# S5 chunk states and outputs: inputs and states as the stationary operand, tables as the moving one

## The chip, the cores and the metric

The kernel runs on one NeuronCore of a Trainium2 chip. The metric is the device time of one launch in microseconds (us). Three runs of the kernel before took 1204.42 to 1205.73 us, median 1205.5.

The engines are named as the profile names them: PE is TensorE (matrix products), PEld its weight loads, DVE is VectorE, ACT is ScalarE, POOL is GpSimd, SP is the engine that issues the loads from memory. In a matrix product one operand is stationary (it is loaded into the array as weights, [contracted rows, output rows]) and the other is moving (it streams past, one column after another).

## The reference

Four layers on x of 256 tokens by 1024 channels, each a token mixer followed by a squared-ReLU MLP of width 4096, both with a pre-norm and a residual addition. Layers 0 and 3 mix with S5, layer 1 with differential attention, layer 2 with pooling. S5, cut to what matters here (64 groups of 16 channels, 64 complex states each; the scan runs over tokens):

```python
u = h @ w_in                                   # 256 x 1024, read as 64 groups of 16 channels
# for each group g and token t, x complex with 64 entries:
#   x[t] = abar * x[t-1] + bbar @ u[t]
y = jnp.einsum('btgp,ghp->btgh', xr, c_re) - jnp.einsum('btgp,ghp->btgh', xi, c_im)
y = y + d_skip * u
z = jax.nn.gelu(y)
z = z * jax.nn.sigmoid(z @ w_gate)
return z @ w_out
```

## The kernel before, in words

**Chunks of four tokens.** The kernel doesn't scan over 256 tokens. It cuts them into 64 chunks of 4. For a pair of groups (2 x 16 channels) an input column holds the 4 x 32 = 128 inputs of one chunk, so a pair has a matrix V of 128 rows by 64 chunks. With tables that are built from the parameters: S (`st`) leads from the inputs of a chunk to the state that the chunk adds (128 = two groups x 64 states, once for the real and once for the imaginary part); T leads from the inputs to the outputs of the same chunk; O leads from the state before the chunk to the outputs. The states are carried from chunk to chunk by VectorE: a rotation by phases (`ph`) makes the recurrence real, two TENSOR_TENSOR_SCAN instructions run it, and a rotation back gives h, the state before each chunk.

**Quarters.** The 32 pairs of groups are taken in four quarters of eight pairs. The steps for a quarter q, each one letter: g the product with W_in (two halves of the contracted dimension), V the scaling and the transposes into V, m (`s5_state`) the chunk states, c (`s5_chain`) the carries, y (`s5_out`) the outputs and the Gelu, z (`s5_z`) the transposes of z into rows of channels. For a half n of the columns e is the product with W_gate (four units) and w that with W_out. The tables: p parameters, i input table, o output table, s phases and decays, S the transposes that make `st` (`states`, copies in L598), T the products that make T (`outputs`, L613 to L626), and f transposes of x.

Layer 0 makes all its tables beside its own work. Those of layer 3 are made during the MLPs ahead, in pieces, and are kept in memory; K, H and L (`s5_get`) bring back the tables of m, of c and of y by loads that SP issues. There are two buffers each of `st`, O and T (q even, q odd), so a table of quarter q can be written when the stage of quarter q - 2 that reads it is over.

**The order** of the steps is written out by hand in the strings `SEQ[0]` and `SEQ[1]` (L87 to L89; layers 0 and 3); every engine gets its instructions in that order. A step's instructions stand in the engines' lists at the place of the step, so an instruction that waits holds up what stands behind it on its engine. Weights come in half blocks of 256 x 512 (or whole 128 x 1024 pieces) that SP loads ahead in the order of use, and that ScalarE and VectorE split into a rounded part and the rest (`fetch`); three products of these parts make one product in float32's precision. The products of m, y, S and T are plain float32 products instead: in the trace each is two PE instructions. All matrix products are recorded under L142, transposes on PE under L146, VectorE's two-operand arithmetic under L151.

**The stages that the change touches.** m makes 16 products per quarter, for each pair j and each of the two parts ri, with 128 columns of `st` stationary (they lie 64 bytes apart) and the 64 columns of V[j] moving:

```python
self.mm(ps[:, 64 * j:64 * j + 64], self.st[q % 2][:, :, 2 * j + ri], V[:, :, j], start=True, stop=True)
```

y makes, for each pair, one product with T[j] stationary (128 columns) and V[j] moving, and two with O stationary (64 columns, one group each) and h moving. The two O products write rows 0 to 63 and 64 to 127 of the same columns, that is they use the two column halves of the array:

```python
self.mm(o, tb["T"][:, j].rearrange("p g x -> p (g x)"), V[:, :, j], start=True, stop=False, ...)
for g in range(2):
    self.mm(o[64 * g:64 * g + 64], tb["O"][:, j, g], tb["h"][:, g, j], start=False, stop=g == 1, ...)
```

The outputs then have rows of outputs and columns of chunks; the Gelu writes them as they are, and two VectorE transposes of 32 x 32 blocks (in `s5_out`) and four PE transposes (in `s5_z`) turn them into the operand of the gate. The chain reads the states from two PSUM banks: two products of 128x1024 with the phases (three planes: minus sine, cosine, sine), one addition of 128x1024, two scans, two products of 128x1008, and four additions of 64x504 that also move the states of one group together into the layout that O wants.

## Time and profile before

| | |
|---|---|
| device time, median of 3 runs | 1205.5 us (1204.42 to 1205.73) |
| span of the profiled execution | 1204.5 us |
| PE busy, share of the span | 1171.1 us, 97% |
| DVE busy | 809.9 us, 67% |
| ACT busy | 663.4 us, 55% |
| PE's share of the chain that ended last | 94% |
| layer 0, m0 to y3 | 38.45 to 145.54 us |
| layer 3, m0 to y3 | 878.50 to 969.35 us |

The profile is one execution; the profiler's span of it, 1204.5 us, stands beside runs of 1204.42 to 1205.73 us. Two stretches of it, given by their start and end in the last lines, hold the stages that the change touches. A share of busy time says which engine had most to do, the chain that ended last says on which engine the end was waiting, step by step, from the last instruction back to the first. [...]

### The profile page before, as it was taken

To read this page: it belongs to the slowest core of one execution; us is meant where nothing else is said; L and a number is where in the kernel's file an instruction comes from. 1 tells how busy PE (TensorE), PEld (TensorE's weight loads), DVE (VectorE), ACT (ScalarE), POOL (GpSimd) and SP (SyncE) were. 2 spreads that over 40 slices of the span, in tenths; PEclk is the share of its full clock that TensorE was granted. 3 is DMA by queue.
4 is the path that set the end of the run, shared out by engine and by line. 5 is a ranking of instruction groups with operands and counts; after the bars stand their busy time and mean duration, and the time that the engine had idled before them with its cause. 6 is when DMAs were issued, how large, how long until landed. Compare 5 with 4: busy or idle time off the path is not lost.

```text
span 1204.5 us, 18922 instructions
## 1 busy us (share of the span) xinstructions
PE 1171.1 (97%) x7192; PEld 1042.7 (87%) x7192; DVE 809.9 (67%) x1488; ACT 663.4 (55%) x1322; POOL 52.3 (4%) x111
## 2 busy tenths in 40 slices
PE   5999999999999999999999999999999999999994
PEld 4989889899888788989888899899898889989983
DVE  7766579857658997986655765655764766655563
ACT  4846367656656676775644754544630156554452
POOL 4002000000000001000000100000100001000000
PEclk9877799999999999999999999999985799999998
DMA  5211256766665444667667365665542256556651
GB/s 150 88 35 36 84 179 188 228 219 208 207 208 168 140 143 154 198 207 217 192 189 232 98 201 180 186 185 185 174 132 79 89 172 195 183 182 189 183 185 58
DMA packets 56635, 196.51 MB, mean 163 GB/s; under 512 B 7136, under 2 KB 7648, under 8 KB 56544
## 3 DMA queue, kind: packets, MB, share of 16 engines
q1 hardware_dynamic: 54528, 189.69, 50.5%
q10 hardware_dynamic: 2016, 5.61, 1.4%
q8 instruction: 56, 0.92, 0.3%
q14 instruction: 35, 0.29, 0.1%
HBM read 188.46 MB, written 6.82 MB: 162 GB/s over the span
## 4 chain that ended last, share of the span: by engine, by line
PE 94%; ACT 2%; DMA 1%; DVE 1%; issue 0%; SPq 0%; POOL 0%; ACTq 0%; POOLq 0%
PE mlp_ps L142 60%; PE mix_ps L142 31%; PE mix_ps L146 2%; DMA start_raw<-in_wts 1%; ACT start_st L598 0%; PE mlp_ps L146 0%; ACT mix_m L885 0%; ACT start_T L626 0%; ACT start_T L623 0%; DVE mix_m L151 0%; SPq L1071 0%; ACT mlp_m L1170 0%; DVE start_x L151 0%; ACT start_ba L575 0%; ACT mix_m L794 0%
## 5 line engine op out<-in xcount | busy, mean ns | idle before, releaser
L151 DVE TENSOR_TENSOR mlp_wlo<-mlp_raw,mlp_whi 128x512 fp32r<-128x512 f32 x492 | 318.5, 686 | 215.9 <-ACT mlp_whi L204 215.7
L204 ACT CAST mlp_whi<-mlp_raw 128x512 fp32r<-128x512 f32 x492 | 281.5, 618 | 255.3 <-PE mlp_ps L142 190.9
L142 PE MATMUL mlp_ps<-mlp_whi,mlp_m 128*128 128x512 f32 x1024 | 327.8, 396 | 0.0
L142 PEld LDWEIGHTS mlp_ps<-mlp_whi,mlp_m 128*128 128x128 f32 x1024 | 192.8, 188 | 45.5
L142 PE MATMUL mlp_ps<-mlp_m,mlp_whi 128*128 128x256 f32 x1248 | 226.2, 283 | 0.0
L142 PE MATMUL mlp_ps<-mlp_wlo,mlp_m 128*128 128x512 f32 x512 | 202.9, 396 | 0.0
L142 PEld LDWEIGHTS mlp_ps<-mlp_m,mlp_whi 128*128 128x128 f32 x1248 | 192.1, 188 | 0.6
L142 PE MATMUL mlp_ps<-mlp_m,mlp_wlo 128*128 128x256 f32 x624 | 175.2, 281 | 0.0
L142 PE MATMUL mlp_ps<-mix_m,mlp_whi 128*128 128x256 f32 x672 | 122.1, 283 | 0.0
L142 PEld LDWEIGHTS mlp_ps<-mlp_m,mlp_wlo 128*128 128x128 f32 x624 | 118.3, 190 | 0.0
L142 PEld LDWEIGHTS mlp_ps<-mlp_wlo,mlp_m 128*128 128x128 f32 x512 | 96.5, 188 | 22.0
L142 PE MATMUL mix_ps<-mix_whi,mix_m 128*128 128x512 f32 (+1 forms) x352 | 108.7, 385 | 0.0
L151 DVE TENSOR_TENSOR mix_wlo<-mix_raw,mix_whi 128x512 fp32r<-128x512 f32 x124 | 81.5, 685 | 38.4 <-ACT mix_whi L204 38.3
L204 ACT CAST mix_whi<-mix_raw 128x512 fp32r<-128x512 f32 x124 | 72.6, 621 | 62.0 <-PE mix_ps L142 35.0
L142 PEld LDWEIGHTS mlp_ps<-mix_m,mlp_whi 128*128 128x128 f32 x672 | 104.5, 188 | 1.8
L142 PE MATMUL mlp_ps<-mix_m,mlp_wlo 128*128 128x256 f32 x336 | 94.5, 281 | 0.0
L142 PEld LDWEIGHTS mix_ps<-mix_whi,mix_m 128*128 128x128 f32 x352 | 66.3, 195 | 13.3 <-issue 0.5
L142 PE MATMUL mix_ps<-mix_wlo,mix_m 128*128 128x512 f32 (+1 forms) x176 | 67.1, 381 | 0.0
L151 DVE TENSOR_TENSOR mlp_m<-mlp_m,mlp_m 128x512 fp32r<-128x512 f32 (+1 forms) x72 | 51.5, 716 | 19.4 <-ACT mlp_m L360 18.6
L142 PEld LDWEIGHTS mlp_ps<-mix_m,mlp_wlo 128*128 128x128 f32 x336 | 63.8, 190 | 0.0
L142 PE MATMUL mix_ps<-mix_m,start_st 128*128 128x64 f32 x256 | 56.9, 398 | 0.4 <-ACT start_st L598 0.3
L142 PEld LDWEIGHTS mix_ps<-mix_m,start_st 128*128 128x128 f32 x256 | 56.4, 311 | 0.9 <-ACT start_st L598 0.9
(324 smaller groups left out, 1523.5 us busy)
## 6 DMA issues: line engine op xcount, KB each, us to landing
mlp_raw<-in_wts SPq DMA_DIRECT2D x252, 512.0 KB, 4.1
mix_raw<-in_wts SPq DMA_DIRECT2D x84, 512.0 KB, 3.6
kept<-mlp_m SPq DMA_DIRECT2D x4, 512.0 KB
start_st<-kept SPq DMA_DIRECT2D x32, 64.0 KB, 3.3
start_x<-in_x SPq DMA_DIRECT2D x4, 256.0 KB
start_raw<-in_wts SPq DMA_DIRECT2D x2, 512.0 KB, 16.8
...
```

Of the source, the lines that this page charges most:

```text
L142: i = self.nc.tensor.matmul(*a, **k)
L146: i = self.nc.tensor.transpose(*a)
L151: (eng or self.nc.vector).tensor_tensor(out=out, in0=a, in1=b, op=op)
L204: nc.scalar.copy(hi[:, s], raw[:, s])
```

## The change

**States.** For each pair j, V[j] (64 columns) is stationary and the table moves: `st`, now laid out as [128, 4, 16, 32], gives the 2 x 128 columns of both parts in one product. Pairs with even j write rows 0 to 63 of the PSUM bank (one column half of the array), pairs with odd j rows 64 to 127. The results have rows of chunks; ScalarE copies them (two copies of 128x512) into `rows`.

**Turn, a new step n** (`s5_turn`): eight PE transposes per quarter turn `rows` into two PSUM banks with rows of states, as the chain reads them.

**Outputs.** V[j] stationary and T[j] moving (128 columns), h stationary and O moving (128 columns, once for each part x); even pairs in one column half, odd ones in the other. Rows are chunks, columns are outputs, and the Gelu writes z in the layout that `s5_z` transposes; the two VectorE transposes go.

**Tables.** O has two halves with zeros for the other group of the pair (so that h of a pair, two groups x 64 states, can be contracted whole): [128, 2, 8, 2, 64], set to zero at the start by GpSimd, and copied by two ScalarE copies of 64x1024 instead of four of 64x512. `ph` has two planes (cosine, sine). The chain uses subtractions instead of the third plane, and its last four additions become two of all 128 rows. V is [128, 8, 64], contiguous per pair. The order of the channels in the inputs (`perm`) is another, and the order strings have the steps n, and m, g, c, e at other places. The diff also drops all comments and docstrings; they and the line numbers are left out here.

```diff
-       0: "f0 g0 p g2 i0 f1 g1 g0 s0 g1 S0 i1 V0 V1 s1 m0 o1 o0 S1 T0 g2 c0 m1 i2 c1 y0 T1 g3 o2 V2 S2 g3 i3 V3 y1 s2 T2 z0 m2 o3 e0 c2 z1 e1 T3 S3 s3 m3 c3 y2 e1 e0 z2 y3 e0 z3 e1 e0 e1 w0 w0 w0 w1 w0 w1 w1 w1",
-       1: "g0 g3 g0 T0 K0 K1 V0 g1 m0 T1 g1 K2 V1 g2 g2 m1 c0 V2 c1 y0 g3 H2 m2 V3 c2 y1 K3 z0 m3 L2 z1 H3 c3 L3 e0 e1 y2 e0 e1 z2 y3 e0 z3 e1 e0 e1 w1 w0 w0 w0 w0 w1 w1 w1"}
+       0: "f0 g0 p g2 i0 f1 g1 g0 s0 g1 S0 i1 V0 V1 s1 m0 o1 o0 S1 n0 T0 m1 c0 g2 n1 i2 c1 y0 T1 g3 o2 V2 S2 g3 i3 V3 y1 s2 T2 m2 z0 o3 e0 n2 c2 z1 e1 T3 S3 s3 m3 e1 n3 c3 y2 e0 z2 y3 e0 z3 e1 e0 e1 w0 w0 w0 w1 w0 w1 w1 w1",
+       1: "g0 g3 g0 T0 K0 K1 V0 g1 m0 T1 g1 n0 K2 V1 g2 m1 c0 g2 n1 V2 c1 y0 g3 H2 m2 V3 y1 n2 K3 c2 z0 m3 L2 z1 H3 e0 n3 c3 L3 e1 y2 e0 e1 z2 y3 e0 z3 e1 e0 e1 w1 w0 w0 w0 w0 w1 w1 w1"}
...
     def s5_state(self, l, P, q, V):
-        tb = P[q]
-        tb["sb"] = []
-        for ri in range(2):
-            ps = self.bank()
-            for j in range(8):
-                self.mm(ps[:, 64 * j:64 * j + 64], self.st[q % 2][:, :, 2 * j + ri], V[:, :, j], start=True, stop=True)
-                self.pe(0.213)
-            tb["sb"].append(ps.rearrange("p (j c) -> p j c", j=8))
+        P[q]["rows"] = S = self.m4([128, 4, 2, 128])
+        for b in range(2):
+            ps = self.bank()
+            for i in range(2):
+                for r in range(2):
+                    j = 4 * b + 2 * i + r
+                    self.mm(ps[64 * r:64 * r + 64, 256 * i:256 * i + 256], V[:, j],
+                            self.st[q % 2][:, :, 2 * j:2 * j + 2].rearrange("p a x c -> p x a c"),
+                            start=True, stop=True, skip_group_check=True)
+                self.pe(0.43)
+            self.nc.scalar.copy(S[:, 2 * b:2 * b + 2].rearrange("p i x m -> p (i x m)"), ps)
+
+    def s5_turn(self, l, P, q):
+        tb = P[q]
+        tb["sb"] = []
+        for ri in range(2):
+            ps = self.bank()
+            for i in range(4):
+                self.tr(ps[:, 128 * i:128 * i + 128], tb["rows"][:, i, ri], self.ident)
+                self.pe(0.113)
+            tb["sb"].append(ps.rearrange("p (j c) -> p j c", j=8))
...
     def s5_chain(self, l, P, q):
...
-            self.tt(m[a], sb[a].unsqueeze(1).broadcast_to(S), turn[:, a:a + 2], ALU.mult)
-        self.tt(m[0], m[0], m[1], ALU.add)
+            self.tt(m[a], sb[a].unsqueeze(1).broadcast_to(S), turn, ALU.mult)
+        self.tt(m[0][:, 0], m[0][:, 0], m[1][:, 1], ALU.add)
+        self.tt(m[1][:, 0], m[1][:, 0], m[0][:, 1], ALU.subtract)
...
-        for g in range(2):
-            for x in range(2):
-                p = slice(64 * g, 64 * g + 64)
-                self.tt(h[64 * x:64 * x + 64, g, :, 1:64], m[0][p, x, :, w], m[1][p, x, :, w], ALU.add)
+        self.tt(h[:, 0, :, 1:64], m[0][:, 0, :, w], m[1][:, 1, :, w], ALU.subtract)
+        self.tt(h[:, 1, :, 1:64], m[1][:, 0, :, w], m[0][:, 1, :, w], ALU.add)
...
     def s5_out(self, l, P, q, V):
...
-        for j in range(8):
-            o = ps[:, 64 * j:64 * j + 64]
-            self.mm(o, tb["T"][:, j].rearrange("p g x -> p (g x)"), V[:, :, j], start=True, stop=False,
-                    skip_group_check=True)
-            for g in range(2):
-                self.mm(o[64 * g:64 * g + 64], tb["O"][:, j, g], tb["h"][:, g, j], start=False, stop=g == 1,
+        for i in range(4):
+            o = [ps[64 * r:64 * r + 64, 128 * i:128 * i + 128] for r in range(2)]
+            for r in range(2):
+                j = 2 * i + r
+                self.mm(o[r], V[:, j], tb["T"][:, j].rearrange("p g x -> p (g x)"), start=True, stop=False,
                         skip_group_check=True)
-            self.pe(0.43)
-        Z = self.m2([128, NT, 8, 32])
-        nc.scalar.activation(out=Z.rearrange("p t j c -> p j t c"),
-                             in_=ps.rearrange("p (j t c) -> p j t c", j=8, t=NT), func=AF.Gelu_apprx_tanh)
-        z = self.m2([128, NT, 2, 128])
-        for t in range(NT):
-            nc.vector.transpose(out=z[:, t].rearrange("p k (j h) -> p j k h", j=8),
-                                in_=Z[:, t].rearrange("p j c -> p (j c)"))
-        tb["z"] = z
+            for x in range(2):
+                for r in range(2):
+                    j = 2 * i + r
+                    self.mm(o[r], tb["h"][:, x, j], tb["O"][:, :, j, x], start=False, stop=x == 1,
+                            skip_group_check=True)
+            self.pe(0.65)
+        tb["z"] = z = self.m2([128, 4, 8, 16])
+        nc.scalar.activation(out=z.rearrange("p s j h -> p j s h"), in_=ps.rearrange("p (j s h) -> p j s h", j=8, s=4),
+                             func=AF.Gelu_apprx_tanh)
...
-        for x in range(2):
-            yield
-            self.halves(lambda g, p: nc.scalar.copy(O[64 * x:64 * x + 64, :, g],
-                                                    d[p, :, x, 1:5].rearrange("p j k h -> p j (k h)")))
+        yield
+        self.halves(lambda g, p: nc.scalar.copy(O[p, g].rearrange("p j x k -> p (j x) k"),
+                                                d[p].rearrange("p j x k h -> p (j x) (k h)")[:, :, 16:80]))
...
-        ph = self.t([128, 3, 8, 64], "ph", 2)
-        nc.scalar.activation(out=ph[:, 0], in_=f, func=AF.Sin, scale=-turn)
-        nc.scalar.activation(out=ph[:, 1], in_=a, func=AF.Sin, scale=-turn, bias=self.hpi[:, 0:1])
-        nc.scalar.activation(out=ph[:, 2], in_=f, func=AF.Sin, scale=turn)
+        ph = self.t([128, 2, 8, 64], "ph", 2)
+        nc.scalar.activation(out=ph[:, 0], in_=a, func=AF.Sin, scale=-turn, bias=self.hpi[:, 0:1])
+        nc.scalar.activation(out=ph[:, 1], in_=f, func=AF.Sin, scale=turn)
...
-        self.st = [self.t([128, 128, 16], f"st{b}") for b in range(2)]
-        self.O = [self.t([128, 8, 2, 64], f"O{b}") for b in range(2)]
+        self.st = [self.t([128, 4, 16, 32], f"st{b}") for b in range(2)]
+        self.O = [self.t([128, 2, 8, 2, 64], f"O{b}") for b in range(2)]
         self.T = [self.t([128, 8, 2, 64], f"T{b}") for b in range(2)]
-        for a in (self.ba[0], self.T[0], self.ba[1], self.T[1]):
+        for a in (self.ba[0], self.T[0], self.O[0], self.ba[1], self.T[1], self.O[1]):
             nc.gpsimd.memset(a, 0.0)
```

**PE in layer 3, from m1 to y0, before.** The rows are PE's instructions in their order; `st_18` is the table `st` of quarter 1, `T_21` and `O_19` are T and O of quarter 0, `mix_ps` are PSUM banks, `mix_whi` and `mix_wlo` parts of weights, and xN counts like instructions in a row.

```order
L142 MATMUL mix_ps_9267<-mix_whi_9223,mix_m_1632_9000 128x256
L142 MATMUL mix_ps_9267<-mix_wlo_9224,mix_m_1632_9000 128x256
L142 MATMUL mix_ps_9267<-mix_whi_9223,mix_m_1633_9001 128x256
L142 MATMUL mix_ps_9326<-mix_m_1666_9261,start_st_18_96 128x64 x8
L142 MATMUL mix_ps_9335<-mix_m_1666_9261,start_st_18_96 128x64 x8
L142 MATMUL mix_ps_9386<-mix_m_1653_9139,start_T_21_99 128x64
L142 MATMUL mix_ps_9386<-mix_m_1680_9356,start_O_19_97 64x64 x2
...
L142 MATMUL mix_ps_9058<-mix_whi_9270,mix_m_1632_9000 128x256
```

The same place now:

```order
L143 MATMUL mix_ps_9292<-start_st_18_96,mix_m_1679_9252 64x256 x4
L143 MATMUL mix_ps_9298<-start_st_18_96,mix_m_1679_9252 64x256 x4
L143 MATMUL mix_ps_9258<-mix_whi_9204,mix_m_1642_8986 128x256
...
L147 MATMUL mix_ps_9347<-start_ident_65,mix_m_1685_9291 128x128 x4
L147 MATMUL mix_ps_9352<-start_ident_65,mix_m_1685_9291 128x128 x4
L143 MATMUL mix_ps_9380<-start_T_21_99,mix_m_1663_9125 64x128 x2
L143 MATMUL mix_ps_9380<-start_O_19_97,mix_m_1693_9317 64x128 x4
...
L143 MATMUL mix_ps_9044<-mix_whi_9261,mix_m_1642_8986 128x256
```

Sixteen products of 64 columns became eight of 256; the second half of W_in for quarter 2 (24 instructions like the third row) moved behind m1, the eight transposes n1 are new, and y0 follows them directly.

**DVE in layer 0, around the transposes of V0 and V1, before.** `q_pa` and `q_pb` are powers that the output tables o1 and o0 are multiplied with, `cad` the sums of those products, `q_tau` the phases of quarter 1.

```order
L151 TENSOR_TENSOR mix_m_137_478<-start_m_7_75,mix_q_pa_269 128x1024
L151 TENSOR_TENSOR mix_m_123_424<-mix_m_123_424,mix_m_124_425 128x1024
L151 TENSOR_TENSOR mix_m_138_479<-start_m_7_75,mix_q_pb_270 128x1024
L151 TENSOR_TENSOR mix_m_140_490<-start_m_7_75,mix_q_pa_269 128x1024
L151 TENSOR_TENSOR mix_cad_475<-mix_m_137_478,mix_m_138_479 128x16x64
L795 STREAM_TRANSPOSE mix_m_125_431<-mix_m_126_432 128x256 x2
L151 TENSOR_TENSOR mix_m_141_491<-start_m_7_75,mix_q_pb_270 128x1024
L795 STREAM_TRANSPOSE mix_m_127_437<-mix_m_128_438 128x256 x2
L151 TENSOR_TENSOR mix_m_129_443<-start_chunk_82,mix_q_tau_294 128x512
L151 TENSOR_TENSOR mix_cad_487<-mix_m_140_490,mix_m_141_491 128x16x64
```

The same place now:

```order
L152 TENSOR_TENSOR mix_m_123_425<-mix_m_123_425,mix_m_124_426 128x1024
L802 STREAM_TRANSPOSE mix_m_125_432<-mix_m_126_433 128x8x32 x2
L802 STREAM_TRANSPOSE mix_m_127_438<-mix_m_128_439 128x8x32
L152 TENSOR_TENSOR mix_m_129_444<-start_chunk_82,mix_q_tau_296 128x512
L802 STREAM_TRANSPOSE mix_m_127_438<-mix_m_128_439 128x8x32
L158 TENSOR_SCALAR mix_m_130_445<-mix_m_129_444 128x512
L152 TENSOR_TENSOR mix_m_129_444<-mix_m_129_444,mix_m_130_445 128x512
L152 TENSOR_TENSOR mix_m_138_473<-start_m_7_75,mix_q_pa_271 128x1024
L152 TENSOR_TENSOR mix_m_139_474<-start_m_7_75,mix_q_pb_272 128x1024
L152 TENSOR_TENSOR mix_m_141_483<-start_m_7_75,mix_q_pa_271 128x1024
L152 TENSOR_TENSOR mix_cad_470<-mix_m_138_473,mix_m_139_474 128x16x64
```

The six instructions that make the output tables of quarters 1 and 0 (the last two follow directly) stood for the most part ahead of V1's transposes; now all six stand behind them.

**ACT in layer 0, from y1's Gelu to the copy of z0, before.** L623 (L621 now) are T's masks, the 8x2x32 (8x4x16 now) activation is the Gelu, L753 (L760 now) the copy of z, L575 (L573 now) copies of the input table of quarter 3, L626 (L624 now) T's shifts, L659 to L665 (L656 to L661 now) the phases of quarter 2.

```order
L623 ACTIVATE start_T_21_99<-mix_ps_798,start_gmask_83 32x8x64
L725 ACTIVATE mix_m_188_777<-mix_ps_752 128x8x2x32
L623 ACTIVATE start_T_21_99<-mix_ps_798,start_gmask_83 32x8x64
L753 COPY mix_m_198_826<-mix_ps_821 128x512
L575 COPY start_ba_16_94<-mix_m_183_739 64x64x16 x2
L626 COPY start_T_21_99<-start_T_21_99 32x16x48
```

The same place now:

```order
L621 ACTIVATE start_T_21_99<-mix_ps_793,start_gmask_83 32x8x64
L680 COPY mix_m_201_816<-mix_ps_817 128x512
L573 COPY start_ba_16_94<-mix_m_188_738 64x64x16 x2
L624 COPY start_T_21_99<-start_T_21_99 32x16x48
L656 ACTIVATE mix_m_196_780<-mix_m_194_778 128x512
L661 ACT_TABLE_LOAD
L661 ACTIVATE mix_ph_785<-mix_m_194_778 128x512
L660 ACTIVATE mix_ph_785<-mix_m_196_780,start_hpi_88 128x512
L624 COPY start_T_21_99<-start_T_21_99 32x16x32
L624 COPY start_T_21_99<-start_T_21_99 32x16x16
L680 COPY mix_m_201_816<-mix_ps_823 128x512
L760 COPY mix_m_205_834<-mix_ps_829 128x512
```

The copy of z stood right behind the second mask; now eleven rows stand between, the two copies of m2's `rows` (L680) among them.

## Rows read from the trace of the kernel before

**Rows 1.** The page: busy time of each engine (1), and the chain's shares (4).

```profile
PE 1171.1 (97%) x7192; PEld 1042.7 (87%) x7192; DVE 809.9 (67%) x1488; ACT 663.4 (55%) x1322; POOL 52.3 (4%) x111
...
PE 94%; ACT 2%; DMA 1%; DVE 1%; issue 0%; SPq 0%; POOL 0%; ACTq 0%; POOLq 0%
```

**Rows 2.** Windows: us; busy PE, PEld, DVE, ACT, POOL (xcount); PEclk; DMA share, GB/s.

```profile
38.45:145.54 107.09, 105.47 (x621) 93.11 (x621) 71.50 (x88) 58.33 (x89) 8.64 (x9) 0.76 0.15 51
878.50:969.35 90.85, 90.85 (x524) 82.03 (x524) 55.15 (x69) 17.27 (x31) 0.38 (x3) 0.73 0.31 104
895.47:898.32 2.85, 2.85 (x27) 2.85 (x25) 2.84 (x5) 0.00 (x0) 0.13 (x1) 1.00 0.04 13
884.00:885.50 1.50, 1.50 (x8) 1.43 (x7) 0.00 (x0) 0.00 (x0) 0.00 (x0) 0.50 0.00 0
399.76:404.81 5.05, 5.05 (x37) 3.90 (x37) 4.78 (x16) 4.06 (x12) 0.00 (x0) 1.00 0.39 158
969.35:972.00 2.65, 2.65 (x15) 2.53 (x16) 0.77 (x2) 0.60 (x1) 0.00 (x0) 0.50 0.73 224
93.97:103.70 9.73, 9.73 (x41) 9.36 (x42) 7.34 (x12) 9.61 (x14) 5.74 (x2) 0.68 0.01 2
```

**Rows 3.** Windows of the eight m (with their sum), then of the eight y.

```profile
878.50:885.55 7.05, 7.05 (x35) 6.93 (x33) 2.64 (x4) 1.14 (x2) 0.00 (x0) 0.86 0.27 77
...
934.29:941.12 6.83, 6.83 (x33) 6.83 (x33) 6.79 (x8) 0.59 (x1) 0.13 (x1) 0.50 0.41 154
sum 55.38, PE 55.38 PEld 55.26 DVE 34.42 ACT 27.28 POOL 5.65; mean PE 6.92 PEld 6.91 DVE 4.30 ACT 3.41 POOL 0.71
...
62.07:70.28 8.21, 8.21 (x49) 6.33 (x50) 1.23 (x1) 0.00 (x0) 0.00 (x0) 0.50 0.00 0
...
964.39:969.35 4.96, 4.96 (x48) 3.90 (x48) 3.09 (x5) 3.10 (x6) 0.00 (x0) 0.95 0.74 230
sum 53.55, PE 53.55 PEld 41.52 DVE 26.28 ACT 10.32 POOL 0.13; mean PE 6.69 PEld 5.19 DVE 3.29 ACT 1.29 POOL 0.02
```

**Rows 4.** Timeline of PE: start us, us, engine line operation out<-in xcount.

```profile
107.38 3.62 PE L142 MATMUL mix_ps<-mix_m,mix_raw 128*128 128x256 f32 x16
110.93 1.97 PE L142 MATMUL mix_ps<-mix_cad,start_ba 128*32 128x64 f32 x32
...
885.55 3.62 PE L142 MATMUL mix_ps<-mlp_cad,start_ba 128*32 128x64 f32 x32
...
905.79 0.48 PE L142 MATMUL mix_ps<-mix_m,start_O 128*64 128x64 f32 x4
...
905.79 0.38 PE L142 MATMUL mix_ps<-mix_m,start_O 128*64 128x64 f32 x2
```

**Rows 5.** The chain that ended last: start us, us, what (eight PE transposes).

```profile
25.34 0.87 PE mix_ps L146 x8
```

**Rows 6.** Timeline of ACT in layer 0.

```profile
37.34 3.69 ACT L598 COPY start_st<-mix_ps 128x512 f32<-128x512 f32 x4
...
95.61 0.56 ACT L753 COPY mix_m<-mix_ps 128x512 f32<-128x512 f32 x1
```

**Rows 7.** Timeline of DVE in layer 3, the chain of quarter 3.

```profile
943.36 2.35 DVE L151 TENSOR_TENSOR mix_m<-mix_ps,mix_ph 128x1024 f32<-128x1024 f32 x2
945.75 1.23 DVE L151 TENSOR_TENSOR mix_m<-mix_m,mix_m 128x1024 f32<-128x1024 f32 x1
947.01 2.34 DVE L697 TENSOR_TENSOR_SCAN mix_m<-mix_rho,mix_m 128x512 f32<-128x512 f32 x2
949.27 2.30 DVE L151 TENSOR_TENSOR mix_m<-mix_m,mix_ph 128x1008 f32<-128x1008 f32 x2
951.60 2.75 DVE L151 TENSOR_TENSOR mix_m<-mix_m,mix_m 64x504 f32<-64x504 f32 x4
```

**Rows 8.** Timeline of DVE in layer 0, up to V1's transposes.

```profile
30.74 1.21 DVE L151 TENSOR_TENSOR mix_m<-start_m,mix_q_pa 128x1024 f32<-128x1024 f32 x1
...
37.12 0.81 DVE L795 STREAM_TRANSPOSE mix_m<-mix_m 128x256 f32<-128x256 f32 x2 [0.45 <-ACT mix_m L794]
```

More of the change, by code (lines that the diff above doesn't have):

```diff
@@ L504, in s5_params @@
         self.tt(fi, t[2], t[3], ALU.subtract)
-        self.cmul(pr[:, 1], pi[:, 1], pr[:, 2], pi[:, 2], pr[:, 3], pi[:, 3], [sm(f"v{q}") for q in range(4)])
+        self.cmul(pr[:, 1], pi[:, 1], pr[:, 2], pi[:, 2], pr[:, 3], pi[:, 3], [sm(f"f{q}") for q in range(4)])
         yield
@@ L737, in s5_z @@
         pt = self.bank()
-        o = pt.rearrange("p (g t a k c) -> p g t a k c", g=2, t=NT, a=2, k=2)
-        for t in range(NT):
-            for k in range(2):
-                self.tr(o[:, :, t, :, k], z[:, t, k], self.ident)
-                self.pe(0.113)
+        o = pt.rearrange("p (a s c) -> p a s c", a=4, s=4)
+        for k in range(4):
+            self.tr(o[:, :, k], z[:, k].rearrange("p j h -> p (j h)"), self.ident)
+            self.pe(0.113)
         ks = slice(2 * (q % 2), 2 * (q % 2) + 2)
```

41 lines of the change are left out of this document (20 added, 21 removed).

## The prediction

> **What bounds the kernel now.** I read the page first: TensorE is busy for 97% of the span, and the chain that ended last is 94% TensorE [rows 1]. So time falls where TensorE gets less to do, up to the point where another engine is late. I then cut the span by stage [rows 2]. The change works in two stretches, each from the start of m0 to the end of y3: 38.45 to 145.54 us in layer 0 (107.09 us, granted clock 0.76) and 878.50 to 969.35 us in layer 3 (90.85 us, clock 0.73). In layer 3 TensorE is busy all of that time and VectorE 55.15 us; in layer 0 VectorE has 71.50 us and ScalarE 58.33 us, because the tables are built there too.
>
> Within the stretches I read the eight m and the eight y stages [rows 3]. An m takes 6.92 us in the mean of eight and 7.05 in m0 of layer 3: 32 instructions, 0.22 us each, weight loads beside them almost without a gap, and no longer at a clock of 0.50 (6.83, m3 of layer 3) than at 0.86. Products of 64 columns (the other product with the input table) run 0.06 us apart at full clock, 32 in 1.97 us [rows 4]; so m waits for its loads, 128 columns taken from the table 64 bytes apart, and streams little. [...] A y takes 8.21 us right behind an m and 4.96 where the clock is nearly whole, and after y3 of layer 3 the clock is 0.50 until 972.00 [rows 2, 3].
>
> **The change part by part.** *States (m).* Out go 16 products of 64 columns a quarter; in come 8 of 256 columns with 64 columns of weights, four to each half of the array. A product is two instructions. A 256-column float32 instruction takes 0.216 us: 16 of them fill 3.62 us with the last one's 0.38 us of run-out [rows 4]. The two halves side by side make that 8 x 0.216 = 1.73.
>
> Do the halves run side by side? The kernel before uses them already, for O: the timeline from 905.790 to 905.801 shows two such instructions that take 0.38 us together, and the four of a pair take 0.48 at 1.2 GHz [rows 4]. There 64 columns take 0.107 (32 in 3.62 us [rows 4]); one behind the other the four would need 3 x 0.107 + 0.38 = 0.70, two by two 0.107 + 0.38 = 0.49. So yes, at 64 columns; at 256 and 128 no row shows it.
>
> Entering and leaving the halves may cost something. A whole-clock y does it 16 times; 4.96 us less 32 steps of 0.06 leaves 3.0, at most 0.19 for a change. The new stages change twice each, so between 0 and 0.38; I take 0.12 for m and 0.2 for y (an estimate), so m is 1.85 us.
>
> *Turn (n).* New: eight transposes a quarter, 0.87 us [rows 5], and ahead of them two ScalarE copies of 128x512, 0.56 each as z's [rows 6] (0.92 as those into the strided table, four in 3.69, is the other end).
>
> *Outputs (y).* Still 24 products, now of 128 columns, 12 to a half, so 24 instructions a half of half of 0.216: 2.65, with the 0.2 2.85 us instead of 6.69 (mean of eight). [...]
>
> *Chain (c).* VectorE's two products from PSUM 2.35, two scans 2.34 and two products 2.30 stay [rows 7]. The 1024-wide addition becomes two of 512, together as long (1.23); four half-height additions (2.75) become two of full height (half, 1.37): 9.6 us instead of 11.0. Two transposes of Z go, on ScalarE a Sin and two O copies, all beside other work. Before, the chain hid under TensorE's work of 8 to 15 us; with less of that it shows, and is what is late next.
>
> *Layer 3, walked from m0's start.* m 1.85, T1 1.97, half of W_in 2.85 [rows 2], n0 0.87: 7.5; from the end of n0 on I count anew. c0 begins with n0's first bank, and half a transpose of V (0.4) stands in it, so h is there at 9.9. TensorE arrives at 2.85 + 1.85 + 2.85 + 0.87 = 8.4 (W_in half, m1, W_in half, n1) and waits 1.5; y0 ends at 12.7. c1 follows with 0.4 + 9.6 + 0.4, so at 20.3; TensorE has 4.7 to do, waits 2.9, y1 ends at 23.1. n2 at 24.0, c2 at 33.5; z0, m3, z1, a gate half of 3.5 (16 instructions of 256 columns), n3 and another gate half bring TensorE to 34.6: no wait, y2 ends at 37.4, two gate halves at 44.9 with z2, c3 has been done since 43.1, y3 ends at 47.7. 7.5 + 47.7 = 55.2 against 90.85: 35.6 less. A wait of 2.9 may lower the clock: minus 2. After y3 the clock no longer starts at 0.50 [rows 2]: plus 1.3. Layer 3 gives **35**. SP's queue: y0 and y1 free O and T earlier, so the loads H2, L2 and K3 follow earlier, and the one weight block behind them is used over 10 us later.
>
> *Layer 0.* Here the order of VectorE and ScalarE matters more. VectorE made most of the six products for the output tables o1 and o0 before V1's transposes at 37.12, the third from 30.74 on [rows 8]. Now all six stand behind V1's transposes and three small rows, from 39.4, 1.14 each, to 46.2. T0 needs the last; its masks on ScalarE wait for four O copies until 49.1, and the addition to T, inside c0 in VectorE's order, is done at 50.8. c0's other 8.3 end at 59. So y0 ends at 61.9 instead of 70.28 [rows 3]; T1, its masks, five products of i2 and c1 lead to y1's end at 76.2. T2 ends at 78.2, and then ScalarE holds the path: in front of z0's copy, without which the gate can't start, it now has nearly the list that ran from 93.97 to 103.70, 9.61 us busy (two masks, Gelu, z's copy, two input-table copies, T's shifts, Abs, a table load, Sins) [rows 2, 6]. One Sin less (0.6), two row copies more (1.1): 10.3, and 0.3 to hand over, so 88.8, TensorE idle from 80.5. A gate half to 92.3 (94 at a lowered clock), z1, gate half 99.4, T3, S3 103.2, m3 in two pieces because its last input-table copy stands behind T's shifts, to 107.9, gate 111.4, n3 112.3, y2 115.1, gate and z2 119; c3 with two weight differences ends at 122.7, y3 at 125.5, with the clock low behind that wait 127. Before 145.54: **18.5** less.
>
> Together 53.5. The profiled execution spans 1204.5, the median of three runs is 1205.5, one above it; from the median I get **1152 us**.
>
> **Rivals.** *The halves' loads are not hidden.* In a column half each load could wait for the stream before it, 64 columns or 0.055 us an instruction: 0.44 for an m and 1.3 for a y. In layer 3 m1 and m2 hide in waits, y1's wait takes in y0's part, 4.7 stay; in layer 0 4: **1161**. For it: O's rows stream too little to show a load behind a stream. Against it: full-array products of 256 columns follow each other at 0.12 (24 in 2.85) with loads beside them all the time [rows 2]. [...]
>
> *The halves stream in turn.* m 3.58 and y 5.4: in layer 3 no wait is left, and the same walk gives 67.6, so 23.3 less; in layer 0 y0 to y3 and m3 carry 11 more, so 8 less. **1174**. For it: nothing at these widths is in the trace; against it, O's pair.
>
> *Layer 0 gains nothing*, because ScalarE and VectorE, which I walked with unit prices, lose another 18 us to waits on each other: **1170**. For it: TensorE's own work there falls to some 63 us, below VectorE's 71.50 less the savings.
>
> *Slower: turns and a lowered clock together.* If the halves stream in turn and half-filled arrays leave the clock at 1.2 GHz, m costs 16 x 0.427 = 6.8, n 1.74, y 48 x 0.22 = 10.5: 19.1 a quarter against 13.6, so 44 us over eight quarters, **1249**. It decides once m, n and y exceed 13.6. Against it: attention's products on row halves of the array ran at a clock of 1.00 (399.76 to 404.81) [rows 2].
>
> **How the numbers follow.** The forecast has 0.63, loads not hidden 0.14, streaming in turn 0.10, a layer 0 without gain 0.08, slower 0.03, and 0.02 that waits elsewhere eat it all. The forecast's own range is 1139 to 1159. Low: half of the idle times I walked (1.5, 2.9, 8.3, 3.7 and some 4.6 ahead of y0 in layer 0, in all 21) could go, with 3 of clock losses. High: row copies at 0.92 instead of 0.56 put 1.4 ahead of m0 and m3 of layer 0 together, twice over with their waits 2.8, and y0 and T1 there at 1.2 GHz add 2.4 and 1.65. To 1174 the range takes in the first three rivals. Faster by over 0.2% (2.4 us, about what a measurement here can tell) 0.95, within it 0.02, slower 0.03.
>
> **What would show it.** Right: m near 1.85 us with pairs of instructions begun together, y near 2.85, clock 1.00 through both; TensorE idle for VectorE ahead of y0 and y1 of layer 3 and ahead of y3 of layer 0, and 8 us for ScalarE ahead of layer 0's first gate half; MLPs and attention unchanged. Wrong: m at 3.5, a clock of 0.50 through y, layer 3's stretch over 60 us, or layer 0's over 95.

## The result, and the profile after

Four runs of the changed kernel took 1160.3 to 1166.0 us, median 1163.2, beside 1204.96 us for the kernel before in the same session: a ratio of 0.9654 (95% interval 0.9634 to 0.9675). The predicted time was 1152 us. The gain is 42 us where the sum had 53.5, so the time lies in the stated range, but above the forecast's own (1139 to 1159): it is inside because the range took in rivals up to 1174. Of the times that the prediction gave, the nearest is not the forecast's but that of the rival "the halves' loads are not hidden", 1161; the times of the single stages below rule that rival out.

The page of the changed kernel, its busy times and the chain's shares, beside [rows 1]:

```profile
PE 1101.5 (95%) x7128; PEld 973.4 (84%) x7128; DVE 792.4 (68%) x1464; ACT 658.0 (57%) x1312; POOL 57.9 (5%) x113
...
PE 84%; DVE 8%; ACT 3%; DMA 2%; POOL 1%; issue 1%; SPq 0%; DVEq 0%; ACTq 0%; POOLq 0%
```

TensorE lost 70 us of busy time and the span 42: the difference is idle time that was not there before. VectorE now has 8% of the chain (1% before). Windows (us; busy PE, PEld, DVE, ACT, POOL; granted clock, PEclk in the rows, as a share of full speed; DMA share, GB/s): the two stretches from m0 to y3, then m0 of layer 3, y2 and y1 of layer 0, the first gate half of layer 0, and the time behind y3 of layer 3.

```profile
39.91:134.12 94.21, 72.53 (x588) 59.83 (x588) 69.23 (x80) 54.99 (x88) 11.85 (x10) 0.88 0.20 60
867.52:924.33 56.81, 52.25 (x493) 44.76 (x492) 43.52 (x54) 17.93 (x32) 0.38 (x3) 1.00 0.51 147
...
867.52:869.40 1.88, 1.88 (x17) 1.06 (x17) 1.17 (x3) 1.62 (x3) 0.00 (x0) 1.00 0.51 81
120.37:123.14 2.77, 2.77 (x49) 2.60 (x48) 2.77 (x4) 0.00 (x0) 0.00 (x0) 1.00 0.61 192
77.13:81.19 4.06, 4.06 (x44) 3.89 (x45) 4.06 (x6) 2.09 (x2) 0.00 (x0) 0.62 0.06 25
93.66:99.00 5.34, 5.34 (x16) 4.38 (x17) 0.00 (x0) 3.57 (x5) 0.00 (x0) 0.66 0.01 3
926.70:932.00 5.30, 5.26 (x31) 5.26 (x32) 1.31 (x3) 1.88 (x5) 0.00 (x0) 0.68 0.75 198
```

An m takes 1.88 us instead of 6.92, a y without a wait 2.77, and layer 3 holds a clock of 1.00 where it had 0.73. That is the change as it was meant. Cut at the ends of the stretches, the span's 42.4 us come from: layer 0 up to the end of y3, 145.54 before and 134.12 now, 11.4; what lies between y3 of layer 0 and m0 of layer 3, 0.4 longer; layer 3's stretch, 90.85 against 56.81, 34.0; and what lies behind it, 235.15 against 237.77, 2.6 lost. (Before, y3 of layer 3 in fact ends at 969.61, 0.26 us behind the cut of [rows 2]; cut there, the last two are 34.3 and 2.9.)

The timeline of TensorE shows the new waits (start us, us, engine line operation out<-in xcount, then the idle time before and what ended it): y0, y1, the first gate half and the second half of m3 in layer 0, y0 of layer 3, y3 of layer 0, and the gate half behind y3 of layer 3.

```profile
59.13 1.10 PE L143 MATMUL mix_ps<-start_O,mix_m 128*64 128x128 f32 x8 [2.84 <-DVE mix_m L152]
...
77.13 1.12 PE L143 MATMUL mix_ps<-start_O,mix_m 128*64 128x128 f32 x8 [2.30 <-POOL mix_rho L665]
...
93.66 0.80 PE L143 MATMUL mix_ps<-mix_m,mix_raw 128*128 128x256 f32 x1 [8.03 <-ACT mix_m L760]
...
112.07 1.98 PE L143 MATMUL mix_ps<-start_st,mix_m 128*64 128x256 f32 x8 [2.39 <-ACT start_st L596]
...
886.84 0.94 PE L143 MATMUL mix_ps<-start_O,mix_m 128*64 128x128 f32 x7 [2.58 <-DVE mix_m L152]
...
130.01 0.44 PE L143 MATMUL mix_ps<-start_O,mix_m 128*64 128x128 f32 x4 [2.28 <-DVE mix_m L152]
...
925.81 0.38 PE L143 MATMUL mix_ps<-mix_m,mix_whi 128*128 128x256 f32 x1 [1.37 <-ACT mix_m L758]
926.74 0.58 PE L143 MATMUL mix_ps<-mix_m,mix_whi 128*128 128x256 f32 x1 [0.54 <-DVE mix_m L152]
```

Note what follows a wait in layer 0: y1 at a clock of 0.62, the gate half at 0.66. From its first O product on y1 takes 4.06 us where y2 takes 2.50, and a gate half that would be 3.55 takes 5.34.

### The profile page after: what moved, and what is told of

Read it like the earlier page. It is cut to its first block, busy times and chain, and to the rows that moved or that the text cites. A ratio compares the mean times of both kernels' runs of the same rounds, so it can differ in the third digit from the quotient of the medians.

```text
span 1162.1 us, 18758 instructions
## 1 busy us (share of the span) xinstructions
PE 1101.5 (95%) x7128; PEld 973.4 (84%) x7128; DVE 792.4 (68%) x1464; ACT 658.0 (57%) x1312; POOL 57.9 (5%) x113
## 4 chain that ended last, share of the span: by engine, by line
PE 84%; DVE 8%; ACT 3%; DMA 2%; POOL 1%; issue 1%; SPq 0%; DVEq 0%; ACTq 0%; POOLq 0%
PE mlp_ps L143 63%; PE mix_ps L143 20%; DVE mix_m L152 5%; DMA start_raw<-in_wts 1%; PE mix_ps L147 1%; DVE mix_m L708 1%; POOL mix_dd L152 1%; ACT start_T L624 1%; DVE mix_wlo L152 1%; ACT start_T L621 0%; PE mlp_ps L147 0%; ACT mix_m L894 0%; DMA mix_raw<-in_wts 0%; SPq L1080 0%; DVE mix_cad L152 0%
## 5 line engine op out<-in xcount | busy, mean ns | idle before, releaser
L205 ACT CAST mlp_whi<-mlp_raw 128x512 fp32r<-128x512 f32 x492 | 281.4, 617 | 260.2 <-PE mlp_ps L143 203.2
L205 ACT CAST mix_whi<-mix_raw 128x512 fp32r<-128x512 f32 x124 | 72.5, 621 | 60.8 <-PE mix_ps L143 32.5
L361 ACT CAST mlp_m<-mlp_m 128x512 fp32r<-128x512 f32 x64 | 39.7, 620 | 23.6 <-DVE mlp_m L152 23.6
L152 DVE TENSOR_TENSOR mlp_m<-mlp_m 128x512 f32<-128x512 f32 x64 | 43.9, 688 | 6.2 <-ACT mlp_m L359 6.0
```

The costliest lines, as they stand in the source:

```text
L152: (eng or self.nc.vector).tensor_tensor(out=out, in0=a, in1=b, op=op)
L205: nc.scalar.copy(hi[:, s], raw[:, s])
L361: nc.scalar.copy(oh, s)
```

## The experiments

All are compared by their ratio to the kernel before in their own session; a ratio's interval is about 0.002 to either side, 2.4 us. The stretches (m0 to y3) are read from each one's trace, which is one execution. They repeat in layer 3 (56.8 to 56.9 in four kernels with the same steps there), less so in layer 0: *z2_early* and *gate_split* have the change's layer 0, begin m0 1.3 us earlier and end y3 0.3 us later, so that theirs is 95.8. *m alone* and *y alone* have the new order of steps too; neither was run with the old one.

| kernel | time, us | ratio | layer 0, TensorE busy in it | layer 3, TensorE busy in it |
|---|---|---|---|---|
| before | 1205.5 | 1 | 107.1, 105.5 | 90.9, 90.9 |
| m alone | 1183.8 | 0.9827 | 101.4, 84.5 | 71.7, 67.3 |
| y alone | 1172.9 | 0.9729 | 91.8, 87.6 | 74.0, 74.0 |
| in turn | 1172.4 | 0.9728 | 98.5, 79.6 | 65.2, 62.5 |
| the change | 1163.2 | 0.9654 | 94.2, 72.5 | 56.8, 52.3 |
| old order | 1162.6 | 0.9623 | 86.7, 68.4 | 64.4, 55.7 |
| reordered | 1142.0 | 0.9478 | 77.0, 67.0 | 56.9, 53.9 |

### Do the halves stream side by side?

```diff
 # s5_state, in each bank
-            for i in range(2):
-                for r in range(2):
+            for r in range(2):
+                for i in range(2):
 # s5_out: first the four pairs with r = 0 (T, O, O each), then those with r = 1
```

> The changed kernel, with the products of m and y issued one column half after the other (within a bank all of half 0, then all of half 1) in place of alternating. Theory 'side by side' (the pairs gain because two halves stream at once): m 3.5 to 3.6 us instead of 1.88, y 5.3 instead of 2.77; in layer 3 the waits for the chain go, its stretch 67 to 69 us instead of 56.8, in layer 0 some 6 to 10 us more; 1179 to 1187 us. Rival 'the loads set the pace' (64-column weight loads, one at a time, whatever the half): m and y as now, 1161 to 1166 us.

1172.43 us, 0.9728 [0.971, 0.9747]: between the theory's time and the rival's. y did what the one said, m what the other said. Windows of the kernel in turn, one m of layer 3 and y2 of layer 0:

```profile
870.26:872.18 1.92, 1.92 (x17) 1.22 (x16) 1.21 (x3) 1.63 (x3) 0.00 (x0) 1.00 0.24 81
...
122.46:127.47 5.01, 5.01 (x50) 4.84 (x49) 5.01 (x7) 2.10 (x4) 0.00 (x0) 1.00 0.32 106
```

y takes 5.01 instead of 2.77: with 24 instructions of one half behind each other, each takes 0.108, and the second half stands idle until its own come. So the pairs do gain by streaming at once. m stayed at 1.92, because there only four instructions of one half stand behind each other, and TensorE starts on the other half's while they wait: the trace has two instructions begun together (0.44 us for both), where two of one half would follow each other at 0.216, and the first of the other half stands four further on in the program.

```profile
870.26 0.44 PE L143 MATMUL mix_ps<-start_st,mix_m 128*64 128x256 f32 x2
```

The same 0.44 is what the changed kernel has at 867.52. A run of four in one half costs next to nothing, a run of 24 nearly all. The eight y lost 2.2 us each, 18 in all; the two stretches grew by 12.7, since the chain and ScalarE's list had left TensorE idle anyway, and 3.8 came back behind layer 3's y3, where a y of 5 us covers what a y of 2.77 doesn't (see the end of layer 3). The time rose by 9.

### What each half of the change is worth

*m alone* is the kernel before with the new `s5_state`, `s5_turn`, `st` and V, and the new order; `s5_out`, O, the chain and z are as before.

> The kernel before with the new m, the step n, the new table layout and the new order of steps, but y, O, the chain and z as before. Theory 'm lowers the clock': without the load-bound m the old y runs at a clock near 1.00 and takes 4.95 us eight times; m and n take 2.9 of the 6.9: 8 x 4.0 + 8 x 1.7 = 46 us less work on TensorE, of which waits for the longer old chain (11.0 us) take back 10 to 15: 1168 to 1178 us. Rival 'the old y lowers the clock by itself': y stays near 8.2 us, the clock 0.50 behind it, 1180 to 1190 us.

1183.82 us, 0.9827 [0.9806, 0.9848]. The time is the rival's, its mechanism only in part. Windows of layer 3's stretch, its y2, y1 and y3, then of layer 0's stretch, and the timeline at y0 of layer 3:

```profile
874.27:945.93 71.66, 67.26 (x494) 56.16 (x493) 53.69 (x68) 20.96 (x38) 0.38 (x3) 0.87 0.39 127
928.24:933.20 4.96, 4.96 (x49) 3.88 (x48) 4.81 (x5) 0.00 (x0) 0.00 (x0) 1.00 0.28 106
910.08:915.60 5.52, 5.52 (x50) 4.29 (x48) 0.89 (x2) 1.08 (x3) 0.00 (x0) 0.89 0.00 0
940.65:945.93 5.28, 5.28 (x51) 4.10 (x49) 2.63 (x6) 2.29 (x5) 0.00 (x0) 0.92 0.60 213
...
38.53:139.88 101.35, 84.49 (x588) 68.45 (x588) 77.36 (x90) 57.98 (x99) 4.45 (x10) 0.83 0.20 60
```

```profile
894.34 0.44 PE L142 MATMUL mix_ps<-mix_m,start_O 128*64 128x64 f32 x2 [3.54 <-DVE mix_m L151]
895.65 0.47 PE L142 MATMUL mix_ps<-mix_m,start_O 128*64 128x64 f32 x2 [0.87 <-DVE mix_m L151]
```

Without the old m the old y of layer 3 takes 4.96 to 5.52 us where it doesn't wait, not 8.2. But only y2 keeps a clock of 1.00: in y1 and y3 the clock falls in the last pairs with no wait ahead of them, to 0.89 and 0.92 in the mean, and the twelve transposes behind y1 take 2.5 us instead of 1.5. So the old m was not alone in lowering the clock. What was missing above all is time in which to hide the old chain: y0 waits 3.54 and 0.87 us for it, and then runs slowly: from 896.06 a pair takes 1.03 us, in y2 0.62. TensorE had 21 us less to do in layer 0 (105.5 to 84.5) and the stretch shrank by 5.7.

*y alone* is the changed kernel with m as before, from the old table layout.

> The changed kernel with m as before (table stationary, 64 columns of V moving, the old table layout, no step n). Theory 'm lowers the clock': m 6.9 us, the clock at 0.50 behind it, y 5.3 to 5.5 us where it follows an m and 2.8 elsewhere, T products and W_in halves behind an m at half speed; 1183 to 1192 us. Rival 'the clock is not m's': y 2.8 us everywhere, clock over 0.9 over the stretch of layer 3, 1170 to 1178 us.

1172.9 us, 0.9729 [0.9714, 0.9743]. Windows of the stretch of layer 3, its m0, the T product behind it, and y1:

```profile
862.13:936.13 74.00, 74.00 (x526) 70.39 (x524) 47.15 (x59) 16.37 (x29) 0.38 (x3) 0.84 0.40 123
862.13:869.16 7.03, 7.03 (x35) 6.92 (x33) 2.66 (x4) 1.14 (x2) 0.00 (x0) 0.73 0.30 83
869.16:872.49 3.33, 3.33 (x33) 3.24 (x33) 2.52 (x3) 0.00 (x0) 0.00 (x0) 0.55 0.35 97
902.84:907.29 4.45, 4.45 (x49) 4.28 (x48) 4.30 (x5) 0.00 (x0) 0.12 (x1) 0.61 0.00 0
```

Again the rival's time, but the clock is m's: 0.73 over m, 0.55 in the T product behind it (3.33 us instead of 1.90), 0.61 in y1, which stands behind another m. The other y of layer 3 have a W_in or gate half ahead of them, which takes the loss, and run in 2.77. The rival's clock over 0.9 was 0.84.

The two together are the lesson of the pair. Alone, y is worth 32 us and m 21; together they are worth 42. With m as before, TensorE is busy in all of layer 3's stretch; add the new m and n, and it has 22 us less to do there and finishes 17 earlier. In layer 0 the new m took 15 us off TensorE (87.6 to 72.5) and the stretch did not get shorter at all (91.8 and 94.2).

### Where layer 0's time went

*The zero column of h* on VectorE instead of GpSimd:

```diff
-        nc.gpsimd.memset(h[:, :, :, 0:1], 0.0)
+        nc.vector.memset(h[:, :, :, 0:1], 0.0)
```

> The changed kernel, the zero column of h (128x16) set by VectorE instead of GpSimd. Theory 'GpSimd holds up y1': in layer 0 GpSimd's product for T2's diagonal takes 9.52 us, and the column behind it comes 1.7 us after VectorE's last addition of c1; without it y1's O products start 1.5 to 1.8 us earlier, and the ScalarE list behind T2 with them: 1160.5 to 1162 us. Rival 'the wait is for something else that ends then' (O1's copies or the chain itself): y1's wait stays over 2 us, 1163 us.

1160.08 us, 0.9622 [0.9605, 0.9639]; the intervals of the two ratios overlap, so the time alone doesn't settle it. The timeline of GpSimd in the changed kernel shows the cause:

```profile
67.48 9.52 POOL L152 TENSOR_TENSOR mix_dd<-start_ident,start_dsk 32x256 f32<-32x256 f32 x1 [10.57 <-DVE start_T L152]
76.96 0.12 POOL L716 MEMSET mix_m<- 128x16 f32 x1
```

GpSimd's product for T2's diagonal (`dd`, in `outputs`) stands ahead of c1's column and takes 9.52 us. VectorE's last addition of c1 ends at 75.4, the column comes at 77.1. With the column on VectorE, y1's wait in TensorE's timeline is 1.04 and 0.94 us follow, no longer 2.30 and 1.12:

```profile
76.31 0.94 PE L143 MATMUL mix_ps<-start_O,mix_m 128*64 128x128 f32 x8 [1.04 <-DVE mix_m L152]
```

y1 takes 4.7 us with its wait instead of 6.8, at a clock of 1.00. So the theory holds for y1, and layer 0's y3 ends at 132.6 instead of 134.1. (Here y0 too ran at full clock; its own column had not been late before, so that isn't put down to the edit.)

*z0 earlier* in the order of layer 0:

```diff
-y1 s2 T2 m2 z0 o3 e0 n2
+y1 z0 s2 T2 m2 o3 e0 n2
```

> The changed kernel, the step z0 of layer 0 written ahead of s2, T2 and m2, so that on ScalarE z0's copy stands ahead of T2's masks and the eight instructions behind them. Theory 'ScalarE's list holds the first gate half': TensorE's idle 8.03 us ahead of it goes; in its place n2 waits 2 to 4 us for m2's second row copy, which still stands behind T2's shifts and the Sins; y3 of layer 0 ends 4 to 6 us earlier, 1157 to 1159.5 us. Rival 'the layer's tables set the pace' (T3, S3 and what VectorE makes for them): the idle time moves to n2 and m3 in full, 1162 to 1164 us.

1158.67 us, 0.9598 [0.9582, 0.9614], clear of the change. In the changed kernel ScalarE's timeline had this ahead of z0's copy (the last row):

```profile
85.30 2.09 ACT L573 COPY start_ba<-mix_m 64x1024 f32<-64x1024 f32 x2
87.42 0.83 ACT L624 COPY start_T<-start_T 32x768 f32<-32x768 f32 x1
...
88.92 1.28 ACT L661 ACT_TABLE_LOAD   x1
...
91.48 1.03 ACT L624 COPY start_T<-start_T 32x512 f32<-32x512 f32 x2
92.53 0.58 ACT L680 COPY mix_m<-mix_ps 128x512 f32<-128x512 f32 x1
93.01 0.59 ACT L760 COPY mix_m<-mix_ps 128x512 f32<-128x512 f32 x1
```

With z0 early the gate half starts right behind m2, and TensorE's timeline shows the next wait, for the row copy that stands behind the same list:

```profile
87.00 3.72 PE L143 MATMUL mix_ps<-mix_m,mix_raw 128*128 128x256 f32 x16
...
95.21 2.35 PE L147 MATMUL mix_ps<-start_ident,mix_m 128*128 128x128 f32 x10 [4.27 <-ACT mix_m L680]
```

8.03 us went and 4.27 came; the stretch is 88.9 instead of 94.2 us. The wait is the expected one, a little over its 2 to 4 us; y3 ends 3.9 us earlier, a little under the 4 to 6.

*The old order*, each n directly behind its m, in both layers and then in layer 0 alone:

```diff
 # layer 0, the part behind y1 and the end
-y1 s2 T2 m2 z0 o3 e0 n2 c2 z1 e1 T3 S3 s3 m3 e1 n3 c3 y2 e0 z2 y3 e0 z3
+y1 s2 T2 z0 m2 n2 o3 e0 c2 z1 e1 T3 S3 s3 m3 n3 c3 y2 e1 e0 z2 y3 e0 z3
```

> The changed kernel with the order of steps of the kernel before, each n directly behind its m. Theory 'the order hides the row copies': each n waits about 1.0 to 1.3 us for ScalarE's copies, in layer 0 more where ScalarE is busy, and c0 of layer 3 hides less; part of it falls into waits that are there anyway: 1167 to 1174 us. Rival 'the order is worth nothing, the chain ends last either way': 1161 to 1165 us.

> The changed kernel, with the old order of steps (each n directly behind its m) in layer 0 alone; layer 3 keeps the new order. Theory 'the new order costs in layer 0 what it gains in layer 3': y3 of layer 0 ends near 125.5 instead of 134.0 us (z0's copy ahead of m2's second row copy, and two gate halves between y2 and y3 to cover c3), layer 3's stretch stays at 56.8: 1153 to 1156 us. Rival 'both stretches move by chance of the profiled execution': 1160 to 1164 us.

The old order in both layers: 1162.6 us, 0.9623 [0.9607, 0.9638], not to be told from the change. My theory was wrong, and "worth nothing" is only the sum. Windows of its stretches:

```profile
38.82:125.48 86.66, 68.40 (x588) 56.09 (x588) 69.05 (x80) 55.05 (x88) 12.90 (x10) 0.92 0.19 57
858.73:923.16 64.43, 55.69 (x494) 47.03 (x493) 46.90 (x59) 20.78 (x37) 0.38 (x3) 0.92 0.47 140
```

The new order gains 7.6 us in layer 3 and loses 7.5 in layer 0. With the old one in layer 0 alone: 1156.68 us, 0.9594 [0.9576, 0.9613], and stretches of 86.8 and 56.9 us; the time is 0.7 us above the theory's range, and y3 of layer 0 ends at 126.7 for its 125.5. ScalarE's list is not avoided by the old order: with z0 ahead of m2 it is n2 that waits, 7.55 us, for its row copy behind that list. But two gate halves (7.0 us) between y2 and y3 cover c3; in the new one a single half does, and y3 waits 2.28 us and then runs at a clock of 0.68.

### The end of layer 3

*z2 one gate half earlier* in layer 3:

```diff
-e1 y2 e0 e1 z2 y3 e0 z3
+e1 y2 e0 z2 e1 y3 e0 z3
```

> The changed kernel, in layer 3 the step z2 written one gate half earlier, so that on ScalarE z2's two copies stand ahead of the split of a weight block that lands only near 924 us. Theory 'z2's copy stands behind a late weight block': TensorE's idle 1.37 us behind y3 goes, and with it the lowered clock behind it: 1.5 to 3.5 us less, 1159.5 to 1161.5 us. Rival 'the gate half after y3 waits for its own weights' (the split's second part, 0.54 us): less than 1 us, 1162 to 1164 us.

1159.9 us, 0.9623 [0.9606, 0.9641]. The interval overlaps the change's, the trace is plain. ScalarE's timeline at the end of layer 3 in the changed kernel: the split of a weight block (L205) waits for its load, and z2's copy (L758) stands behind it.

```profile
924.14 1.14 ACT L205 CAST mix_whi<-mix_raw 128x512 fp32r<-128x512 f32 x2 [7.96 <-DMA mix_raw<-in_wts]
925.18 0.58 ACT L758 CAST mix_m<-mix_ps 128x512 fp32r<-128x512 f32 x1
```

And the window behind y3 with z2 early, no wait and a clock of 1.00:

```profile
924.91:928.05 3.14, 3.14 (x28) 3.14 (x27) 2.59 (x4) 2.50 (x6) 0.00 (x0) 1.00 0.76 223
```

The gate half behind y3 ends 3.0 us after y3 instead of 6.8: a gain of 3.8, of which the waits themselves are 1.9. The lowered clock is not sure to follow them: in *z0_early* and *old_order_layer0*, with the change's steps there and waits of 1.21 and 0.54 us, it doesn't fall, and the gate half ends 5.1 us after y3. So some 2 us of the gain are shown to be the order's, and 1.7 hang on that execution.

*W_gate split in layer 3* (`GW = (512, 0)`), so that its weight blocks give their buffers back earlier.

> The changed kernel, layer 3's first four half blocks of W_gate split into two parts like the rest, instead of used whole. Theory 'the weight block behind the gate is late': a whole block keeps its load buffer until the gate half that reads it is over, so the block for the gate half after y3 lands at 924.1 and z2's copy stands behind its split; with split blocks the buffers come free earlier, the waits of 1.37 and 0.54 us after y3 and the clock of 0.68 behind them go (2.5 to 4 us), and four gate halves take 2.9 instead of 3.5 (2.4 us): 1157 to 1159 us. Rival 'VectorE has no room for four more splits': c2 or c3 end later and y2 or y3 wait 1 to 3 us, 1161 to 1165 us.

1169.05 us, 0.9683 [0.9666, 0.97]. The interval and the change's just touch, but in the trace layer 3's stretch is 65.1 us instead of 56.8: slower. VectorE had no room: one more subtraction of a split stands ahead of c0 and one inside it, and y0 waits 4.85 us instead of 2.58. The larger wait is ahead of the first gate half, in TensorE's timeline:

```profile
912.60 0.58 PE L143 MATMUL mix_ps<-mix_m,mix_whi 128*128 128x256 f32 x1 [5.39 <-DVE mix_m L152]
```

The split operand of z0 needs a subtraction on VectorE; in VectorE's timeline it stands behind 8 us of c2, and the gate half waits for it.

```profile
909.64 2.30 DVE L152 TENSOR_TENSOR mix_m<-mix_m,mix_ph 128x1008 f32<-128x1008 f32 x2
911.86 0.69 DVE L152 TENSOR_TENSOR mix_m<-mix_ps,mix_m 128x512 fp32r<-128x512 f32 x1
```

The rival held in its cause, with more than it asked for and at other places (y0 and the gate half instead of y2 and y3). Behind y3 only 0.22 us of wait is left.

### Together

*combined* is the column, z0, T0 behind c0 in layer 0 (`n0 m1 c0 T0 g2 n1`, since T0's addition held up c0 on VectorE by 2.36 us) and the split of W_gate.

> The changed kernel with four edits: h's zero column on VectorE, z0 early, W_gate of layer 3 split, and T0 of layer 0 behind c0 (so that T0's addition doesn't hold up c0 on VectorE, where it waited 2.36 us). Theory 'four separate waits': the gains add up, 2 to 3 for the column, 4 to 6 for z0, 4 to 6 for the gate, 2 for T0: 1147 to 1152 us. Rival 'one wait takes the place of another': no more than the best of the single edits, 1156 to 1160 us.

1154.78 us, 0.9563 [0.9549, 0.9577]: between theory and rival, because it holds one edit that loses. Its layer 0 takes 78.1 us instead of 94.2, its layer 3 66.5 instead of 56.8.

*reordered* leaves the split out, takes the old end of the order in layer 0 (`m3 n3 c3 y2 e1 e0 z2 y3 e0 z3`) and z2 early in layer 3. *rows_early* also puts m2 ahead of s2 and T2 (`y1 z0 m2 s2 T2 o3 e0 n2`). T0 behind c0 and the old end were not run by themselves.

> The changed kernel with h's zero column on VectorE, in layer 0 z0 early, T0 behind c0 and the old end of the order (both gate halves between y2 and y3), and in layer 3 z2 early; no split of W_gate. Theory 'the lost time of layer 0 is the order on ScalarE, VectorE and GpSimd': y3 of layer 0 ends at 115 to 118 instead of 134.0 us, layer 3's stretch stays at 56.8 and its end loses 1.5 to 3.5: 1142 to 1146 us. Rival 'each wait removed is taken by the next': layer 0 ends no earlier than 125, 1152 to 1156 us.

> The reordered kernel, with m2 of layer 0 also ahead of s2 and T2, so that on ScalarE m2's two row copies stand ahead of T2's masks, the input-table copies, T2's shifts and the Sins. Theory 'n2 waits for the row copies behind that list': TensorE's idle 3.53 us ahead of n2 and the lowered clock behind it (z1 and the gate half 4.87 instead of 3.56) go; c2 needs the phases of s2, now later, so a part comes back as a wait of y2 or m3: 1138 to 1141 us. Rival 'the phases and T2 are then what is late': the wait moves to c2 and y2 in full, 1141.5 to 1144 us.

1142.04 us, 0.9478 [0.9459, 0.9496], and 1139.74 us, 0.9454 [0.9437, 0.9472]. Their windows of layer 0, reordered and then with the rows early:

```profile
39.29:116.25 76.96, 66.98 (x588) 56.49 (x588) 67.65 (x82) 53.71 (x86) 8.04 (x6) 0.93 0.21 63
```

```profile
40.34:113.26 72.92, 64.25 (x589) 54.12 (x589) 67.19 (x83) 54.19 (x87) 11.36 (x6) 0.98 0.21 67
```

Both times lie in the theories' ranges, and y3 of layer 0 ends at 116.25 in *reordered*, in the range too. The matrix products are those of the change in both; the order and one instruction's engine are worth another 21 to 24 us. T0's place is not all gain: y0 now waits 2.60 us for T0's shifts on ScalarE. Between the two last the intervals overlap; in the trace n2's wait of 3.53 us is gone, and what came back is at n3, 2.69 us instead of 1.03, and not at m3 or y2.

## Why the prediction was right, and where not

**The sum.** 53.5 us were forecast and 42.4 came: 7.1 are missing in layer 0, 3.9 behind layer 3's y3 and 0.4 between the layers, and layer 3's stretch gave 0.4 more. The traces give the clock as a share of full speed and show no frequency: what the prediction calls 1.2 GHz is, at O's pair, a granted clock of 0.50 (905.79 to 906.27 of the kernel before). Nor does a run show the range's 2.4 and 1.65 us for y0 and T1 of layer 0 at that clock: y0 ran at 0.62 and took 2.0 more than at full clock, and T1's 32 instructions behind it (63.63) took the 1.97 that 32 of 64 columns took before.

**Right: m, y and n, and the clock where nothing waits.** 1.85 us was forecast for m and 1.88 measured, 2.85 and 2.77 for y, 0.87 for n and 0.79 to 0.97 measured; layer 3 held 1.00. The step from O's pair to 256 and 128 columns held, and *in turn* shows that y is at 5.01 without it. The halves' loads are hidden (in y2 of layer 0 they were busy for 2.60 of the 2.77 us, beside the products), that rival is out: a y of 24 instructions a half at 0.108 is 2.6 us (the sum had 2.65), and 2.77 leaves 0.2 for entering and leaving, what was taken.

**Right: layer 3's stretch.** 55.2 us were walked, 56.8 measured, with waits of 2.58 and 1.86 us where 1.5 and 2.9 stood, none at y2 and y3, as walked. That it agrees this well is in part luck. The walk let c0 begin with n0's first bank; it began at 877.63, 2.6 us after n0, since two transposes of V1 and a weight's subtraction stood ahead of it on VectorE. And the 2 us that were set aside for a lowered clock did not come: no row of the kernel before shows that term, and both waits left the clock at 1.00.

**Wrong: "instead of 0.50 after y3: plus 1.3".** The time behind layer 3's y3 got 2.6 us longer. Before, y3's 4.96 us covered the late weight block and z2's copy behind it; I shortened that cover to 2.8 and did not ask what lay under it. *z2_early* gives it back. The short y3 is not all of it: in *y alone* and *old order*, with a y3 of 2.77 as well, the block's split came 6.8 and 6.7 us after y2's end, not 10.1, and nothing waited. Why the block is late in the change was not tried; those stretches last 74 and 64 us, so its load may simply have more time there.

**Wrong by 7 us: layer 0, 18.5 forecast and 11.4 measured.** By the walk's own marks: y0 ended at 63.6 instead of 61.9 (c0 was done at 59.6 for the walk's 59, the rest is y0's clock; that m0 began 1.5 later than before cost nothing, as *z2_early* shows), y1 at 81.2 instead of 76.2, z0's gate half could start 12.5 us behind that, against 12.6, and from there to y3's end it was 40.5 instead of 38.2. The failed steps are two.
- "T1, its masks, five products of i2 and c1 lead to y1's end" leaves out GpSimd's queue, where the zero column of h stands behind a product that took 9.52 us there. *column_on_vector* took 2.1 us off y1.
- "94 at a lowered clock", "127 with the clock low behind that wait": 3.2 us were allowed for the clock behind waits in layer 0. It took 9.8, over what the same stages have at full clock: from their first O product on y0 took 4.50, y1 4.06 and y3 4.10 (y2 2.50), m3's second half took 1.91 (0.94), and the gate halves behind z0's wait and behind m3's took 5.34 and 5.42 (3.55). The lowered clock stood in the text as an estimate, and at the two places where it was put its size was right: 1.7 and 1.5 us for 1.8 and 1.6 measured. It was left out behind the waits of y0, y1 and m3, where the runs show 2.0, 1.6 and 2.8.

**Half right: ScalarE's list ahead of z0's copy.** Its length was right (8.3 us of idle forecast, 8.03 measured). But the walk saw this wait in the order of the steps and took it as given; moving one step ahead (*z0_early*) removes it, with 4.27 us of another wait in its place.

**The rival "layer 0 gains nothing"** was priced at 18 us of waits. About 7 of them came, and *y alone* against the change shows the kind: in layer 0 the new m is worth nothing in the order given.
